# Earlier loads for the second MLP products, and recurrences placed inside w_o's first pass

## The chip, the cores and the metric

The kernel runs on one core of a Trainium2 chip. The core has a matrix engine (TensorE, PE in the profile; its weight loads are PEld), a vector engine (VectorE, DVE), a scalar engine (ScalarE, ACT), GpSimd (POOL) and SyncE (SP), which issues the DMAs here. The metric is the device time of one execution in microseconds. The kernel before takes 2242.0 us, the median of 3 runs (2241.39 to 2243.5).

## The reference

A trunk of two layers over a sequence of 1024 positions and a model width of 1024, all in float32:

```python
for layer in range(DEPTH):                      # DEPTH = 2
    h = rmsnorm(x, mix_norm_g[layer])
    if layer % 2 == 0:
        x = x + diff_attention(h, ...)          # layer 0
    else:
        x = x + recurrent_block(h, ...)         # layer 1
    x = x + sqrelu_mlp(rmsnorm(x, mlp_norm_g[layer]), mlp_w1[layer], mlp_w2[layer])
return rmsnorm(x, final_norm_g)

def sqrelu_mlp(h, w1, w2):                      # w1: 1024 x 4096, w2: 4096 x 1024
    return jnp.square(jax.nn.relu(h @ w1)) @ w2

def recurrent_block(h, ...):
    gate_branch = gelu(h @ w_y)
    xb = causal_depthwise_conv(h @ w_x, conv_w, conv_b)
    ...
    r, i = sigmoid(...), sigmoid(...)           # gates, block-diagonal products of xb
    log_a = -8.0 * r * softplus(-lam_param)
    a, mult = exp(log_a), sqrt(-expm1(2.0 * log_a))
    u = mult * (i * xb)
    _, hs = lax.associative_scan(_lru_combine, (a, u), axis=1)   # h_t = a_t h_(t-1) + u_t
    return (hs * gate_branch) @ w_o
```

## The kernel before

Every product of float32 matrices is made from rounded parts: each operand is split into a high part (ACT copies it to the rounded type, L342) and a low part (DVE subtracts, L345), and three matmuls (high x high, high x low, low x high) are added up in a result bank. A matmul here has 128 rows and columns of weights and 512 columns of data. Names ending in h and l are the parts: w2h and w2l, ysh and ysl.

The program's stages in the profiled execution are attention (until about 625 us), MLP of layer 0 (first product to 935, second product to about 1240), the recurrent block (to 1585), and the MLP of layer 1 (first product to 1902, second product and final norm to the end).

**The MLP's first product** (`mlp`) goes over 16 pairs of row blocks, `i` from 0 to 15. For each it forms seven products of half-size blocks, as in Strassen's scheme, 12 matmuls each, and DVE adds them up in the tiles ct and cl. The rest of a pair (`hidden_steps`) is done beside the next pair's products: ACT takes relu (rt, rl) and square (st, sl), DVE forms sums (h12, h34), and SP stores the seven half blocks as `hid[i]` to device memory: ct, two parts of cl, then h12 and two parts of h34. After the last pair these steps stand alone. In this stage the order on each engine is that of the code (`manual_schedule`).

**The second product** (`Second`) is cut into slots of 24 matmuls. Slots 0 to 7, of kind P, read half a block row of w2 (one DMA, L71) and two stored half blocks of hid (two DMAs, L91), and `prepare` splits both. `run` loads four slots ahead (AHEAD = 4) and prepares two ahead. Slots 0 and 1 are loaded at the start of pair 15 and prepared in it. In layer 1 the residual is kept transposed: `fetch_x` loads its eight blocks into xm, `turn_x` turns them with transposes on TensorE (L250) during slots 4 to 7, and ACT copies them out (L251). Layer 0 loads rows of x instead (L239).

**The recurrent block** works on pairs of 128 channels, n = 0 to 3. `lru` is the recurrence of one channel block: on ACT T = tanh, exp, sqrt and a copy with three functions that need table loads; on DVE two products, one more, and a scan along the sequence. The result times the gate branch is split into ys. At n = 3 the first pass of w_o is done with ys0 to ys3 (`out_group`: eight result blocks of 24 matmuls, two for each of four groups of w_o's columns), then both recurrences of the last pair, and then the second pass with ys4 to ys7 (L588 to L591), whose results are added to x (L1031) and passed block by block to the norm and splits of layer 1's first product (z, t12, t34, ssacc). Outside `manual_schedule` a scheduler of the framework orders the instructions of each engine.

SP issues the DMAs in its order, and each issue waits for the DMA eight issues before it.

Of the kernel before, what the change touches and what calls it, by code (L numbers as in the profile page):

```python
# [17 lines left out]
S = 1024  # L18
NK = D // P
# [275 lines left out]
class Trunk:  # L295
# [740 lines left out]
        if done is not None:  # L1036
            done(m)

    def out_group(self, blocks, w, r0, done=None, order=tuple(range(NK)), first=None, beside=()):

        nb = len(blocks)
        per = NK // nb
        wt = {} if first is None else {order[0] // per: first}
        beside = iter(beside)
        for m in order:
            g = m // per
            if g not in wt:
                wt[g] = self.w_out(w, r0, nb, g * per * P)
            for _ in self.out_block(blocks, wt[g], m, m % per, done=done):
                pass  # L1050
            next(beside, lambda: None)()

# [111 lines left out]
    def mlp(self, layer, last):  # L1164

        nc = self.nc
        mm = nc.tensor.matmul
        w1, w2 = self.ins["mlp_w1"][layer], self.ins["mlp_w2"][layer]
        self.hid = [self.dram.tile([P, 7, CH], F32, name=f"hid{layer}_{b}") for b in range(16)]
        l, r = slice(0, CH), slice(CH, S)
        box = {}

        def means():
            ps = self.acc1()  # L1180
            for j in range(NT):
                nc.tensor.matmul(ps[:, j : j + 1], self.ssacc[:, j * P : (j + 1) * P], self.ones, start=True, stop=True)
            inv = self.const.tile([P, NT], F32, name=f"inv{layer}")
            nc.vector.tensor_scalar(out=inv, in0=ps[:, :NT], scalar1=1.0 / D, scalar2=EPS, op0=ALU.mult, op1=ALU.add)
            nc.vector.reciprocal(out=inv, in_=inv)
            box["inv"] = inv
            self.ssacc = None

        def add(out, x, y, op=ALU.add):
            nc.vector.tensor_tensor(out=out, in0=x, in1=y, op=op)  # L1190

        with self.tc.manual_schedule(engines={EPE, EACT, EDVE, ESP}):
            second = self.second(w2, box, last)
            raws = self.pair_raws(w1, 1)
            before = {}
            for i in range(16):
                w = self.w
                new = {}
                if i + 1 < 16:
                    new, self.w = self.pair_weights(raws, i + 1)  # L1200
                if i + 2 < 16:
                    raws = self.pair_raws(w1, i + 2)
                if i == 15:
                    second.load(0)
                    second.load(1)
                    second.fetch_x(4)
                top, low = self.t4("ct"), self.t4("cl")
                p1, p67, p53 = self.acc1(), self.acc2(), self.acc2()
                p2, p4 = self.accg(), self.accg()

                def do(*names):
                    for name in names:
                        for steps in (new, before):
                            if name in steps:
                                steps[name]()

                def rows(a, b, bank, k):
                    (ah, al), (bh, bl) = w[a], self.sx[k][b]
                    mm(bank, ah[:, k], bh, start=k == 0, stop=False)  # L1219
                    mm(bank, ah[:, k], bl, start=False, stop=False)  # L1220
                    mm(bank, al[:, k], bh, start=False, stop=k == 3)  # L1221

                def product(a, b, bank):
                    for k in range(4 if i else 0):
                        rows(a, b, bank, k)

                if i == 0:

                    for k in range(4):
                        for at in (("A11", "B11", p1), ("S2", "T2", p67[:, l]), ("S1", "T1", p53[:, l]), ("S4", "B22", p53[:, r]),  # L1230
                                   ("S3", "T3", p67[:, r]), ("A12", "B21", p2), ("A22", "T4", p4)):
                            rows(*at, k)
                product("A11", "B11", p1)
                if "e6" in before:
                    before["e6"]()
                do("th", "s12", "rt", "st")
                product("S2", "T2", p67[:, l])
                nc.scalar.activation(out=top[:, l], in_=p1, func=AF.Copy)
                do("tl", "s34", "rl", "sl")
                product("S1", "T1", p53[:, l])  # L1240
                add(low[:, l], top[:, l], p67[:, l])
                do("h12", "lh", "t12", "l12")
                product("S4", "B22", p53[:, r])
                add(low[:, r], low[:, l], p53[:, l])
                do("h34", "t34", "l34")
                product("S3", "T3", p67[:, r])
                add(top[:, r], low[:, r], p53[:, r])
                do("ll")
                product("A12", "B21", p2)
                both = low.rearrange("p (h c) -> p h c", c=CH)  # L1250
                add(both, both, p67[:, None, r].to_broadcast([P, 2, CH]))
                if i == 2:
                    means()
                if i == 3:
                    box["q"] = box["inv"] if last else self.spread(box["inv"])
                if i == 15:
                    second.prepare(0)
                    second.prepare(1)
                product("A22", "T4", p4)
                add(top[:, l], top[:, l], p2)  # L1260
                before = self.hidden_steps(i, top, low, last)
                before["e6"] = lambda low=low, p4=p4: add(low[:, l], low[:, l], p4, ALU.subtract)
            for name in ("rt", "st", "e6", "rl", "sl", "t12", "t34"):
                before[name]()
            self.sx = None
            second.run()
# [134 lines left out]
    def recurrent(self, done):  # L1401
        nc, ins = self.nc, self.ins
        wx, wy, wo = ins["rec_w_x"][0], ins["rec_w_y"][0], ins["rec_w_o"][0]
        self.xg = self.new_xg
        rb = self.norm_later()
        self.x = [None] * NK
        ys, kept = {}, {}

        def back(c):
            parts = []  # L1410
            for p in range(2):
                t = self.t4("ys", F32R)
                nc.sync.dma_start(out=t.bitcast(F32), in_=kept[c][p])
                parts.append(t)
            return parts

        for n in range(4):
            rg = self.t4("raw", F32, (P, 2, 2, 256), "R")
            for gi, g in enumerate(("rec_w_a", "rec_w_i")):
                nc.sync.dma_start(out=rg[:, gi], in_=ins[g][0, n].rearrange("(k p) m -> p k m", p=P))  # L1420
            wg = self.split(rg, (P, 2, 2, 256), "wg")
            pair = (2 * n, 2 * n + 1)
            xbs, xss = zip(*[self.conv(wx, c, rb) for c in pair])
            gates = [self.gelu2(wy, c, rb) for c in pair]
            if n == 3:
                for c in range(4):
                    ys[c] = back(c)
            parts = []
            for j, c in enumerate(pair):
                sel = slice(j * P, (j + 1) * P)  # L1430
                r = self.gate(wg, 0, xss, sel, "r", self.vec("rec_b_a", c))
                ig = self.gate(wg, 1, xss, sel, "ig", self.vec("rec_b_i", c))
                parts.append((r, ig, c, xbs[j]))
            if n == 3:
                self.out_group([ys[c] for c in range(4)], wo, 0)
            hs = [self.lru(*p) for p in parts]
            for j, c in enumerate(pair):
                nc.vector.scalar_tensor_tensor(out=hs[j], in0=gates[j], scalar=0.5, in1=hs[j], op0=ALU.mult, op1=ALU.mult)
                ys[c] = self.split(hs[j], (P, S), "ys")
                if n < 2:  # L1440
                    kept[c] = [self.dram.tile([P, S], F32, name=f"y{c}{p}") for p in "hl"]
                    for t, d in zip(ys.pop(c), kept[c]):
                        nc.sync.dma_start(out=d, in_=t.bitcast(F32))
        self.out_group([ys[c] for c in range(4, 8)], wo, 512, done, beside=[lambda: self.mlp_first(1)])
        self.w_lo = None


# [83 lines left out]
```

## Time and profile before

| | |
|---|---|
| median of 3 runs | 2242.0 us (2241.39 to 2243.5) |
| profiled execution | 2248.95 us, span 2247.2 us |
| mean granted clock of TensorE | 0.981 |
| busy share of the span | PE 95%, DVE 68%, ACT 48%, POOL 4% |

The span is the time from the first to the last recorded instruction of the profiled execution; its own time is 1.75 us longer. An engine's row in a timeline gives start, duration, line, operation, output and inputs, and in brackets how long the engine had stood idle before it and what ended that. The durations of matmuls overlap: the next one starts before the last has ended. In a table of windows PEclk is the share of full clock that was granted.

### The profile page before, as it was taken

To read this page: it belongs to the slowest core of one execution; us is meant where nothing else is said; L and a number is where in the kernel's file an instruction comes from. 1 tells how busy PE (TensorE), PEld (TensorE's weight loads), DVE (VectorE), ACT (ScalarE), POOL (GpSimd) and SP (SyncE) were. 2 spreads that over 40 slices of the span, in tenths; PEclk is the share of its full clock that TensorE was granted. 3 is DMA by queue.
4 is the path that set the end of the run, shared out by engine and by line. 5 is a ranking of instruction groups with operands and counts; after the bars stand their busy time and mean duration, and the time that the engine had idled before them with its cause. 6 is when DMAs were issued, how large, how long until landed. Compare 5 with 4: busy or idle time off the path is not lost.

```text
span 2247.2 us, 26498 instructions
## 1 busy us (share of the span) xinstructions
PE 2130.8 (95%) x9826; PEld 1758.0 (78%) x9826; DVE 1530.5 (68%) x2073; ACT 1067.6 (48%) x1627; POOL 100.1 (4%) x171
## 2 busy tenths in 40 slices
PE   8997999879999999899999999999899999899997
PEld 7786777768888888788887887777688888688885
DVE  5465676565896777577878477756967776486575
ACT  4344566456663444344435266635644443453343
POOL 3201111110000000000000000000000000000000
PEclk9998999999999999999999999999999999999998
DMA  6635353453634443597647322144244444874633
GB/s 188 175 88 130 97 143 101 123 152 109 211 116 142 155 155 134 190 353 280 218 158 240 90 78 84 36 159 132 94 151 155 150 150 169 322 263 166 217 128 135
DMA packets 239298, 355.82 MB, mean 158 GB/s; under 512 B 16225, under 2 KB 137154, under 8 KB 239170
## 3 DMA queue, kind: packets, MB, share of 16 engines
q1 hardware_dynamic: 230338, 326.87, 43.6%
q0 software_dynamic: 7680, 25.17, 4.8%
q10 hardware_dynamic: 1152, 2.10, 0.3%
q8 instruction: 77, 1.26, 0.2%
q14 instruction: 51, 0.42, 0.1%
HBM read 229.29 MB, written 91.23 MB: 143 GB/s over the span
## 4 chain that ended last, share of the span: by engine, by line
PE 60%; DVE 11%; ACT 7%; issue 3%; DMA 2%; POOL 0%; SPq 0%; ACTq 0%; POOLq 0%; DVEq 0%
PE acc L1219 5%; PE acc L1220 5%; PE acc L1221 5%; PE acc L144 4%; PE acc L145 4%; PE acc L143 4%; PE acg L1219 2%; PE acg L1221 2%; PE acg L1220 2%; PE acc L589 2%; PE acc L588 2%; PE acb L145 2%; PE acb L143 2%; PE acb L144 2%; PE acg L145 2%
## 5 line engine op out<-in xcount | busy, mean ns | idle before, releaser
L1121 ACT ACTIVATE ct<-ct 128x1024 f32<-128x1024 f32 x64 | 67.9, 1061 | 251.1 <-DVE ct L1190 250.1
L345 DVE TENSOR_TENSOR h2l<-h,h2h 128x1024 fp32r<-128x1024 f32 x112 | 136.6, 1220 | 65.6 <-ACT h2h L342 61.9
L766 ACT ACTIVATE p<-acc,nmax 128x768 f32<-128x768 f32 (+7 forms) x128 | 95.3, 744 | 143.1 <-DVE nmax L783 71.5
L588 PE MATMUL acg<-xgh,wh 128*128 128x512 f32 x384 | 161.6, 421 | 1.5 <-ACT vT L732 1.5
L589 PE MATMUL acg<-xgl,wh 128*128 128x512 f32 x384 | 152.7, 398 | 0.0
L591 PE MATMUL acg<-xgh,wl 128*128 128x512 f32 x384 | 152.7, 398 | 0.0
L342 ACT ACTIVATE h2h<-h 128x1024 fp32r<-128x1024 f32 x112 | 117.6, 1050 | 59.6 <-DMA h<-hid 51.3
L342 ACT ACTIVATE w2h<-w 128x1024 fp32r<-128x1024 f32 x80 | 84.3, 1054 | 88.0 <-DVE w L56 72.1
L143 PE MATMUL acc<-w2h,h2h 128*128 128x512 f32 x256 | 103.0, 402 | 13.9 <-ACT w2h L342 12.2
L143 PE MATMUL acc<-h2h,w2h 128*128 128x512 f32 x256 | 101.1, 395 | 7.5 <-ACT w2h L342 7.4
L418 POOL TENSOR_TENSOR rstd<-ms,mhalf 128x4 f32<-128x4 f32 (+2 forms) x25 | 22.4, 897 | 1900.0 <-DVE ms L416 1898.6
L144 PE MATMUL acc<-w2l,h2h 128*128 128x512 f32 x256 | 102.3, 400 | 2.8 <-DVE w2l L345 2.8
L1220 PE MATMUL acc<-t12l,w12h 128*128 128x512 f32 x256 | 100.7, 393 | 4.4 <-DVE t12l L345 4.4
L1190 DVE TENSOR_TENSOR cl<-cl,acc 128x512 f32<-128x512 f32 x64 | 60.8, 950 | 64.3 <-PE acc L1221 64.3
L345 DVE TENSOR_TENSOR w2l<-w,w2h 128x1024 fp32r<-128x1024 f32 x80 | 97.7, 1222 | 9.0 <-PE acc L144 4.9
L145 PE MATMUL acc<-h2h,w2l 128*128 128x512 f32 x256 | 100.9, 394 | 2.7 <-DVE w2l L345 2.7
L1219 PE MATMUL acc<-t12h,w12h 128*128 128x512 f32 x256 | 100.6, 393 | 3.1 <-DVE ct L1190 3.1
L145 PE MATMUL acc<-w2h,h2l 128*128 128x512 f32 x256 | 101.5, 396 | 0.0
L144 PE MATMUL acc<-h2l,w2h 128*128 128x512 f32 x256 | 100.8, 394 | 0.0
L1221 PE MATMUL acc<-t12h,w12l 128*128 128x512 f32 x256 | 100.2, 391 | 0.0
L762 PE MATMUL acc<-ks,qs 128*128 128x512 f32 (+2 forms) x192 | 67.8, 360 | 23.0 <-DMA ks<-qkh 23.0
L591 PEld LDWEIGHTS acg<-xgh,wl 128*128 128x128 f32 x384 | 73.8, 192 | 17.0 <-DVE wl L345 0.5
(383 smaller groups left out, 6004.4 us busy)
## 6 DMA issues: line engine op xcount, KB each, us to landing
w<-in_mlp_w_dram SPq DMA_DIRECT2D x96, 512.0 KB, 4.4
raw<-in_mlp_w_dram SPq DMA_DIRECT2D x64, 512.0 KB, 4.4
h<-hid SPq DMA_DIRECT2D x64, 512.0 KB, 5.2
h<-hid SPq DMA_DIRECT2D x96, 256.0 KB, 5.1
w<-in_mlp_w_dram SPq DMA_DIRECT2D x80, 256.0 KB, 3.9
hid<-cl SPq DMA_DIRECT2D x64, 256.0 KB, 2.3
hid<-h SPq DMA_DIRECT2D x32, 512.0 KB, 2.6
hid<-h SPq DMA_DIRECT2D x64, 256.0 KB, 2.4
```

Source lines behind the costliest of these rows:

```text
L143: mm(bank[m], ah, bh, start=first, stop=False)
L144: mm(bank[m], ah, bl, start=False, stop=False)
L145: mm(bank[m], al, bh, start=False, stop=end)
L342: nc.scalar.activation(out=hi, in_=src, func=AF.Copy)
L345: (lo_eng or nc.vector).tensor_tensor(out=lo, in0=src, in1=hi.bitcast(F32), op=ALU.subtract)
L588: mm(ps[:, pc], a, xh[:, cs], start=(k == 0), stop=False)
L589: mm(ps[:, pc], a, xl[:, cs], start=False, stop=False)
L591: mm(ps[:, pc], b, xh[:, cs], start=False, stop=(k == n - 1))
L766: nc.scalar.activation(out=p[c][:, :n], in_=src, func=AF.Exp, bias=nmax[:, c : c + 1], accum_out=sums[:, c : c + 1])
L1219: mm(bank, ah[:, k], bh, start=k == 0, stop=False)
L1220: mm(bank, ah[:, k], bl, start=False, stop=False)
L1221: mm(bank, al[:, k], bh, start=False, stop=k == 3)
```

## The change

There are three edits. In `mlp` the loads of slots 2 and 3 are issued with pair 15's last steps, before its stores; `fetch_x(4)`, which loads xm0 to xm3 in layer 1, moves behind them; and slot 2 is prepared between pair 15's steps e6 and rl. In `recurrent`, at n = 3, the two recurrences are emitted after the first and the third result block of w_o's first pass. In `out_group`, the second pass is called with `late=2`: the first two result blocks, with another tag for their banks, do their products with ys4 and ys5 first, and those with ys6 and ys7 follow.

```diff
-    def out_group(self, blocks, w, r0, done=None, order=tuple(range(NK)), first=None, beside=()):
+    def out_group(self, blocks, w, r0, done=None, order=tuple(range(NK)), first=None, beside=(), late=0):
...
-            for _ in self.out_block(blocks, wt[g], m, m % per, done=done):
+            if late and m == order[0]:
+                two = [self.out_block(blocks, wt[g], n, n % per, done=done, tag="S") for n in order[:2]]
+                for steps in two:
+                    for _ in range(nb - late):
+                        next(steps)
+            steps = two.pop(0) if late and m in order[:2] else self.out_block(blocks, wt[g], m, m % per, done=done)
+            for _ in steps:
                 pass
...
                 if i == 15:
                     second.load(0)
                     second.load(1)
-                    second.fetch_x(4)
...
                 if i == 15:
                     second.prepare(0)
                     second.prepare(1)
+                    second.load(2)
+                    second.load(3)
+                    second.fetch_x(4)
...
-            for name in ("rt", "st", "e6", "rl", "sl", "t12", "t34"):
+            before["rt"]()
+            before["st"]()
+            before["e6"]()
+            second.prepare(2)
+            for name in ("rl", "sl", "t12", "t34"):
                 before[name]()
...
+            hs = []
+            recurrence = lambda: hs.append(self.lru(*parts[len(hs)]))
             if n == 3:
-                self.out_group([ys[c] for c in range(4)], wo, 0)
-            hs = [self.lru(*p) for p in parts]
+                self.out_group([ys[c] for c in range(4)], wo, 0, beside=[recurrence, lambda: None, recurrence])
+            else:
+                recurrence()
+                recurrence()
...
-        self.out_group([ys[c] for c in range(4, 8)], wo, 512, done, beside=[lambda: self.mlp_first(1)])
+        self.out_group([ys[c] for c in range(4, 8)], wo, 512, done, beside=[lambda: self.mlp_first(1)], late=2)
```

On ACT, around the end of layer 0's first product, the steps of pair 15 (ct, cl) and the splits of slot 2 (the first h2h and w2h after them) and slot 3 stood and stand as follows, the kernel before first:

```order
L1121 ACTIVATE ct_7941<-ct_7941 128x1024 x2
L1121 ACTIVATE cl_7942<-cl_7942 128x1024 x2
L342 ACTIVATE h2h_8105<-h_1308_8091 128x1024
L342 ACTIVATE w2h_8109<-w_1307_8090 128x1024
L342 ACTIVATE h2h_8144<-h_1310_8096 128x1024
```

Here slot 2's two splits stand behind both passes of cl, and slot 3's behind them. In the changed kernel the same place reads:

```order
L1130 ACTIVATE ct_7941<-ct_7941 128x1024 x2
L342 ACTIVATE h2h_8084<-h_1304_8059 128x1024
L342 ACTIVATE w2h_8088<-w_1303_8058 128x1024
L1130 ACTIVATE cl_7942<-cl_7942 128x1024 x2
L342 ACTIVATE h2h_8144<-h_1306_8064 128x1024
```

The two splits of slot 2 moved from behind cl to ahead of it; the count of instructions is the same.

On SP, at the end of layer 1's first product, the stores of pairs 14 and 15 (hid_14, hid_15) and the loads of slots 2, 3 and 4 (w, then two h) stood in this order before, where xm is the residual and gb the gain of the final norm:

```order
L232 DMA xm_14792<-x_0_12316 128x1024
...
L1127 DMA hid_14_12698<-ct_14647 128x512
...
L1127 DMA hid_15_12699<-h_2410_14942 128x512 x2
L1280 DMA gb_14949<-in_final_norm_g_dram 128x1024
L71 DMA w_2414_14951<-in_mlp_w_dram 128x2x512
...
L71 DMA w_2416_14956<-in_mlp_w_dram 128x2x512
...
L71 DMA w_2418_14961<-in_mlp_w_dram 128x2x512
...
L232 DMA xm_14974<-x_4_12320 128x1024
```

All three slots stand behind the stores of pair 15, and xm4 to xm7 behind the three slots. In the changed kernel the order is:

```order
L1136 DMA hid_14_12698<-h_2396_14862 128x512 x2
L71 DMA w_2405_14909<-in_mlp_w_dram 128x2x512
...
L71 DMA w_2407_14914<-in_mlp_w_dram 128x2x512
...
L232 DMA xm_14919<-x_0_12329 128x1024
...
L1136 DMA hid_15_12699<-ct_14792 128x512
...
L1295 DMA gb_14967<-in_final_norm_g_dram 128x1024
L71 DMA w_2422_14969<-in_mlp_w_dram 128x2x512
...
L232 DMA xm_14974<-x_4_12333 128x1024
```

Slots 2 and 3 and xm0 to xm3 now stand between the two groups of stores; slot 4 and xm4 to xm7 stay behind pair 15's.

On ACT, in w_o's first pass, T, r and w are tiles of the two recurrences (r_1944 the first, r_1948 the second), woh the split weights and ysh the split results. The kernel before, from the first split of the second pass's weights on:

```order
L342 ACTIVATE woh_2001_12286<-raw_2000_12284 128x1024
L1390 ACTIVATE T_1992_12252<-r_1944_11928,sp4_895 128x1024
L1391 ACT_TABLE_LOAD
...
L1390 ACTIVATE T_1994_12263<-r_1948_11958,sp4_895 128x1024
L342 ACTIVATE woh_2025_12398<-raw_2024_12396 128x1024
...
L1394 ACTIVATE T_1994_12263<-T_1994_12263 128x1024
L342 ACTIVATE ysh_1996_12275<-r_1944_11928 128x1024
L342 ACTIVATE ysh_1998_12280<-r_1948_11958 128x1024
```

The first recurrence begins only behind woh_2001, a weight of the second pass. In the changed kernel, where woh_1977 and woh_1987 are the third and fourth weight group of the first pass, the rows are:

```order
L1407 ACTIVATE w_1960_12026<-T_1959_12025 128x1024
L342 ACTIVATE woh_1977_12144<-raw_1976_12142 128x1024
L1409 ACTIVATE T_1959_12025<-T_1959_12025 128x1024
L1405 ACT_TABLE_LOAD
L1405 ACTIVATE T_1971_12102<-r_1948_11958,sp4_895 128x1024
...
L1409 ACTIVATE T_1971_12102<-T_1971_12102 128x1024
L342 ACTIVATE woh_1987_12210<-raw_1986_12208 128x1024
L342 ACTIVATE woh_2001_12286<-raw_2000_12284 128x1024
L342 ACTIVATE ysh_1996_12275<-r_1944_11928 128x1024
L342 ACTIVATE ysh_1998_12280<-r_1948_11958 128x1024
```

Both chains moved from behind the weights' splits into the first pass, the first ahead of its third weight group and the second ahead of its fourth.

## Rows read from the trace of the kernel before

**Rows 1.** The page's first part: busy time of each engine, share of the span and count of instructions.

```profile
PE 2130.8 (95%) x9826; PEld 1758.0 (78%) x9826; DVE 1530.5 (68%) x2073; ACT 1067.6 (48%) x1627; POOL 100.1 (4%) x171
```

**Rows 2.** TensorE's list of waits over the whole span: bank and line that waited, what ended it, then us in total, times, longest.

```profile
PE acc L143 <- ACT w2h L342: 19.6, 7, 9.0
...
PE acc L588 <- ACT ysh L342: 5.0, 1, 5.0
PE acc L1220 <- DVE t12l L345: 4.4, 3, 1.7
...
PE acc L1219 <- DVE ct L1190: 3.1, 2, 2.8
```

**Rows 3.** TensorE's timeline in layer 0's second product: its first matmul, the last one of slot 1, the first ones of slot 2 and of slot 8.

```profile
935.40 0.39 PE L143 MATMUL acc<-h2h,w2h 128*128 128x512 f32 x1
...
946.05 0.39 PE L145 MATMUL acc<-h2h,w2l 128*128 128x512 f32 x1
952.94 0.79 PE L143 MATMUL acc<-h2h,w2h 128*128 128x512 f32 x1 [6.50 <-ACT w2h L342]
...
988.56 0.39 PE L143 MATMUL acb<-h2h,w2h 128*128 128x512 f32 x1
```

**Rows 4.** ACT's timeline beside it: pair 15's cl, and the splits of slots 2, 4 and 5.

```profile
938.61 2.14 ACT L1121 ACTIVATE cl<-cl 128x1024 f32<-128x1024 f32 x2
950.89 1.06 ACT L342 ACTIVATE h2h<-h 128x1024 fp32r<-128x1024 f32 x1 [10.14 <-DMA h<-hid]
...
956.33 1.06 ACT L342 ACTIVATE h2h<-h 128x1024 fp32r<-128x1024 f32 x1 [0.70 <-DMA h<-hid]
...
960.33 1.06 ACT L342 ACTIVATE h2h<-h 128x1024 fp32r<-128x1024 f32 x1 [2.00 <-DMA h<-hid]
```

**Rows 5.** SP's timeline beside it: the last stores of pair 14, and the first load of slot 2.

```profile
924.52 5.16 SPq L1127 DMA_DIRECT2D hid<-h  x3
...
944.13 0.63 SPq L71 DMA_DIRECT2D w<-in_mlp_w_dram  x1
```

**Rows 6.** Windows of 2 us: busy time and instructions of each engine, then TensorE's granted clock, the DMA share and GB/s.

```profile
952.00:954.00 2.00, 1.06 (x2) 0.57 (x2) 2.00 (x2) 1.26 (x2) 0.00 (x0) 0.50 1.06 393
1618.00:1620.00 2.00, 2.00 (x6) 1.55 (x5) 1.97 (x4) 1.45 (x2) 0.00 (x0) 0.50 0.85 239
1918.00:1920.00 2.00, 0.00 (x0) 0.00 (x0) 0.00 (x0) 0.00 (x0) 0.00 (x0) 0.50 1.05 407
```

**Rows 7.** TensorE's timeline in w_o's passes: the second pass's first matmul, the last before its wait and the first after it, then the first matmul of layer 1's MLP and the one after that stage's last wait.

```profile
1534.56 0.39 PE L588 MATMUL acc<-ysh,woh 128*128 128x512 f32 x1
...
1542.49 0.39 PE L591 MATMUL acg<-ysh,wol 128*128 128x512 f32 x1
1547.85 1.22 PE L588 MATMUL acc<-ysh,woh 128*128 128x512 f32 x2 [4.97 <-ACT ysh L342]
...
1585.66 0.39 PE L1219 MATMUL acb<-b,wth 128*128 128x512 f32 x1
...
1616.30 0.47 PE L1219 MATMUL acc<-t12h,w12h 128*128 128x512 f32 x1 [2.76 <-DVE ct L1190]
```

**Rows 8.** ACT's timeline from the last gate of the recurrences on: two splits of w_o's weights, and the start of the first recurrence with its first table load and the pass behind it.

```profile
1491.23 1.12 ACT L1377 ACTIVATE ig<-acc,cols 128x1024 f32<-128x1024 f32 x1 [1.60 <-PE acc L591]
...
1513.71 1.06 ACT L342 ACTIVATE woh<-raw 128x1024 fp32r<-128x1024 f32 x1 [7.51 <-DMA raw<-in_rec_w_o_dram]
1523.42 1.06 ACT L342 ACTIVATE woh<-raw 128x1024 fp32r<-128x1024 f32 x1 [8.65 <-PE acc L589]
1524.39 1.14 ACT L1390 ACTIVATE T<-r,sp 128x1024 f32<-128x1024 f32 x1
1525.55 1.28 ACT L1391 ACT_TABLE_LOAD   x1
1526.84 1.15 ACT L1391 ACTIVATE r<-r,nsp 128x1024 f32<-128x1024 f32 x1
```

**Rows 9.** DVE's timeline behind it: the first results of the second pass, the last block's result, and the sum ct of layer 1's MLP.

```profile
1556.62 2.35 DVE L1031 TENSOR_TENSOR x<-x,acc 128x1024 f32<-128x1024 f32 x2 [3.11 <-PE acc L591]
...
1585.86 1.22 DVE L1031 TENSOR_TENSOR x<-x,acc 128x1024 f32<-128x1024 f32 x1
...
1615.48 0.68 DVE L1190 TENSOR_TENSOR ct<-cl,acc 128x512 f32<-128x512 f32 x1
```

**Rows 10.** TensorE's timeline in layer 1's second product: the first matmul, the first of slot 2, the first transposes of slot 4.

```profile
1902.78 0.39 PE L143 MATMUL acc<-w2h,h2h 128*128 128x512 f32 x1
...
1922.85 0.79 PE L143 MATMUL acc<-w2h,h2h 128*128 128x512 f32 x1 [9.03 <-ACT w2h L342]
...
1936.67 0.60 PE L250 MATMUL acb<-ident,xm 128*128 128x128 f32 x4
```

**Rows 11.** ACT's timeline beside it: the split of slot 2, and the first copy of a transposed block.

```profile
1920.80 1.06 ACT L342 ACTIVATE h2h<-h 128x1024 fp32r<-128x1024 f32 x1 [12.67 <-DMA h<-hid]
...
1938.68 0.58 ACT L251 ACTIVATE x<-acb 128x512 f32<-128x512 f32 x1
```

**Rows 12.** SP's timeline beside it: the last stores of pair 14, and the first load of slot 2.

```profile
1891.47 5.58 SPq L1127 DMA_DIRECT2D hid<-h  x3
...
1912.31 0.64 SPq L71 DMA_DIRECT2D w<-in_mlp_w_dram  x1
```

## Prediction

> **What bounds the kernel now.** I read the page's busy line first, then TensorE's list of waits, then the timeline around each long wait, and last the engine or queue that ended it. TensorE is busy 95% of the span [rows 1], so a change can win only where TensorE stands still or runs at half clock. Of the waits, three places are touched by the edits [rows 2]: L143 waiting for w2h (19.6 us in 7 waits, the start of the second MLP products), L588 waiting for ysh (5.0 us, w_o's second pass), and behind it L1220 waiting for t12l (4.4 us) and L1219 for ct.
>
> In both second products TensorE does the first two slots of 24 matmuls back to back and then stops until slot 2's weights are split: in layer 0 from 946.05 to 952.94, in layer 1 until 1922.85 after 9 us [rows 3, 10]. What ends it is ACT's h2h, which itself waited for a DMA [rows 4, 11]. That DMA was issued after pair 15's hid stores, at 944.13 and 1912.31 [rows 5, 12], though SP had finished pair 14's stores at 924.52 + 5.16 = 929.68. In w_o's second pass ACT starts the recurrences at 1524.39, after an early split of the next weights, and the first ysh releases TensorE at 1547.85, 5 us after it ran out of other matmuls at 1542.7 [rows 7, 8].
>
> Each such gap is paid twice. In the windows behind the two MLP gaps, and behind the 2.76 us wait at 1616.30, the granted clock stands at 0.50 of 2.4 GHz, that is 1.2 GHz, after TensorE had stood idle [rows 6]. So I count arrival times of a later matmul against the full pace, which contains both.
>
> **The change part by part.** The pace: 48 matmuls from 935.40 to 946.05, 47 steps, are 0.2266 us each, a slot of 24 is 5.44 us [rows 3].
>
> *A, layer 0's second product.* Slots 2 and 3 are now issued behind pair 14's stores, from 929.7, and their six DMAs have some nine us before pair 15's stores, the first of which waits for ACT's ct, done where cl starts at 938.61 [rows 4]. Slot 2's ACT work (h2h, w2h, 0.96 us apart) goes between ct and cl, so starts at about 938.6 [rows 4]; with the DVE halves it is ready near 942, slot 3 near 947. TensorE needs them at 946.3 and 951.7. Both wait no longer. Price of the move: cl and all of pair 15's stores go 2 x 0.96 = 1.9 us later, and slot 4 stands where slot 2 stood. Its h2h would then run at 950.89 + 1.9 = 952.8 and its w2l end near 956.3, against a need at 935.40 + 4 x 5.44 = 957.2. That is hidden by 0.9 us; uncovered it would cost the shortfall and perhaps a new half clock, 3 to 4 us. The slots after it come each 4.0 us (956.33 to 960.33, [rows 4]), faster than 5.44. So eight slots end at 935.40 + 43.5 = 978.9 in place of 988.56 [rows 3]: 9.7 us. Bounds 6 to 9.7.
>
> *B, the recurrences.* Same instructions, moved. ACT is free from 1491.23 + 1.12 = 1492.35, so the four ACT passes of each recurrence run beside the first pass of w_o. The second ysh needs no more than the split of woh before it (1523.42 in the rows of before), so both are ready near 1527 and their ysl near 1535. late=2 puts 24 matmuls on ys4 and ys5 first, which cover 1534.56 to 1540.0. Nothing is left to wait for, and 192 matmuls end at 1534.56 + 192 x 0.2266 = 1578.1 in place of 1585.66 [rows 7]: 7.6 us.
>
> What is late next is DVE. It is without a gap from 1556.62 to the ct that frees TensorE at 1616.30, 59.5 us of work [rows 9], and TensorE in that stretch loses 4.4 + 2.76 us [rows 2, 7]. With the first block finished after 36 matmuls, at 1542.7, DVE may start near 1543 and have that work done at 1602.6. The order also places about 6.4 us of it ahead of the last block's result, where 30.3 us (1585.86 to 1616.16) stood behind it, so from that side ct ends at 1578.3 + 24.6 = 1602.9. TensorE itself would arrive at 1616.30 - 2.76 - 4.4 - 7.6 = 1601.5. DVE's two limits coincide, so it has no slack while results come in one by one, and I take 3 us of remaining waits: 1604.6, a gain of 11.7, rounded to 11.5. Bounds: 7.5 (all those waits stay) to 15 (none stays).
>
> What the move costs in the first pass: the split of the fourth weight group, at 1513.71 [rows 8], now stands behind both chains on ACT. Adding the rows' durations, 4 table loads of 1.28 and eight passes of about 1.1, two of which (T of L1394) wait for DVE, it lands near 1515 and its wol near 1518.7. TensorE needs it two blocks before the end, at 1534.56 - 10.9 = 1523.7. It is covered by 5 us. The recurrences' passes on DVE (about 1.2 us each like the row at 1585.86, [rows 9]) delay results by up to 2 us; I count nothing, and what it costs if that is wrong is the slower rival.
>
> The trace has a table load from 1525.55 to 1526.83 and the next pass at 1526.84 [rows 8], so nothing follows the load. The Trainium skill (ScalarE: Activation LUTs, What ACT_TABLE_LOAD costs) adds a drain of about 1.38 us to each load. By that rule four loads would take some 5.5 us more and use up the 5 us of cover, and the sum would lose about 0.5 us; the row disagrees and I go by the row.
>
> *C, layer 1's second product.* The same move, with SP free from 1891.47 + 5.58 = 1897.05 [rows 12]. Unhindered, slot 4's transposes start at 1902.78 + 4 x 5.44 = 1924.5 in place of 1936.67 [rows 10]: 12.1 us. But these transposes read xm4 to xm7, which are queued behind pair 15's stores (now 1.9 us later), the final gain and slot 4. Slot 4 takes slot 2's place: 1920.80 + 1.9 = 1922.7 [rows 11]. Four xm are 2.1 MB; at the 407 GB/s of a full window [rows 6] 5.2 us, so they land at 1927.9. TensorE does the xm0 to xm3 quarter (0.44 us) and waits about 3.0. Slot 5's transposes need the banks that ACT's copies (1938.68 in before, behind the next slot's splits, [rows 11]) empty: another 1.5. I take 12.1 - 3.0 - 1.5 = 7.6. Bounds: 12.1 if the data is early, and 3 if TensorE waits twice for 3 us and falls to half clock once more for about 3.
>
> At 407 GB/s the row says that loads can run near that rate. The Trainium skill (DMA: Bandwidth & Descriptors, Where 436 GB/s comes from) has loads from HBM bound at about 358 GB/s. By that rule the xm would land 0.7 us later and C would be 6.9; the row disagrees.
>
> Sum: 9.7 + 11.5 + 7.6 = 28.8 us. Against the profiled execution (2248.95 us, span 2247.2) that is 2220. The median of the runs is 2242.0, 7 us under it; the same amount taken from it gives 2213.
>
> **The rivals.**
> *The wait moves to the DMAs.* For: from 942 and from 1910 on the queues are full (share 1.05 in the window, [rows 6]), and nothing is removed from them. Against: slots are used at 1.05 MB per 5.44 us, half of what the row moves. If slot 4 and the xm are late, A falls to 6, C to 3, and the sum to 20.5: 2221.5.
> *DVE sets the end of B.* For: its 59.5 us without a gap. Against: the order moves work ahead of the last block. If all 30.3 us stay behind it, B is 7.6 and the sum 24.9: 2217.
> *Slower: the recurrences hold up the first pass.* One mechanism: on ACT's queue the split of the fourth weight group waits for the two chains, on DVE the results wait behind the scans. Price: the chains took 29.1 us in before, from T at 1524.39 to 1553.5, where DVE's 3.11 us of idle time before 1556.62 begin [rows 8, 9]. TensorE begins to pay beyond 5 us of delay. If it stood for all of it and 3 us of half clock, B would be 11.5 - 32 = -20.5, and with A and C as forecast the time 2242.0 - 17.3 + 20.5 = 2245; with A and C at 9 together, 2253. For it: the one-engine queues. Against: ACT was idle 7.5 and 8.7 us before the two splits there [rows 8].
> *The loads come no earlier,* since their buffers or slot 2's h wait for something of pair 15: then A and C vanish and a B at its lower end of 7.5 with its stores 2 us late gives 2236; if B fails too, no change.
>
> **How the numbers follow.** Forecast 0.60 (2213, own range 2208 to 2218), DMA 0.20, DVE 0.12, loads no earlier 0.05, slower 0.03. With A 6, B 7.5, C 3 the sum is 16.5 and the time 2225.5; with 9.7, 15 and 12.1 it is 36.8 and 2205. The range is 2205 to 2227. A difference below 0.2%, 4.5 us, is what a measurement of this kernel can't tell from none. Faster 0.94, within 0.03, slower 0.03.
>
> **What would show it.** In the profile after: L143's wait for w2h gone from the 5 to 10 us class in both layers; slot 8 of layer 0 starting 43.5 us after the first matmul; L588's wait for ysh gone and T of L1405 near 1492 relative to the same first pass; a DVE wait at t12l or ct still there, under 4 us; a wait of about 3 us at the transposes of L250. Wrong would be: a new wait at L589 or L591 for wol in the first pass, a wait for w2h at slot 4, or a granted clock of 0.50 at new places.

## The result and the profile after

The changed kernel takes 2217.94 us, the median of 4 runs (2216.23 to 2222.5), against 2242.75 us of the kernel before (4 runs, 2241.39 to 2243.67). The ratio is 0.9893, 95% interval 0.9876 to 0.991. The forecast was 2213, in a range of 2205 to 2227: right in direction and within the range, 5 us optimistic by this median. The same kernel was timed twice more, each time beside the kernel before: 2214.19 us beside 2246.09 (0.9859, interval 0.9836 to 0.9882) and 2217.05 beside 2245.92 (0.9871, 0.9857 to 0.9886). The three gains are 24.8, 31.9 and 28.9 us; forecast were 28.8.

TensorE's list of waits in the changed kernel (bank and line that waited, what ended it, us in total, times, longest), to be laid beside [rows 2]; L1227 and L1228 are L1219 and L1220 of before:

```profile
PE acc L143 <- ACT w2h L342: 4.1, 4, 1.5
PE acc L1227 <- DVE ct L1199: 3.1, 2, 2.8
...
PE acg L250 <- DMA xm<-x: 1.7, 2, 1.0
...
PE acc L1228 <- DVE t12l L345: 0.3, 1, 0.3
```

The wait for ysh is gone, and with it those for t12l but for 0.3 us. L143's wait fell from 19.6 to 4.1 us, its longest from 9.0 to 1.5; what is left of it stands at the end of both second products, where before had it too. New is L250's wait for xm. The wait for ct is what it was.

TensorE's timeline of the changed kernel, answering to [rows 3], [rows 7] and [rows 10]:

```profile
938.68 0.39 PE L143 MATMUL acc<-h2h,w2h 128*128 128x512 f32 x1
...
949.56 0.39 PE L143 MATMUL acc<-h2h,w2h 128*128 128x512 f32 x1
...
982.20 0.39 PE L143 MATMUL acb<-h2h,w2h 128*128 128x512 f32 x1
...
1531.13 0.39 PE L588 MATMUL acc<-ysh,woh 128*128 128x512 f32 x1
...
1574.65 0.39 PE L1227 MATMUL acb<-b,wth 128*128 128x512 f32 x1
...
1600.26 0.77 PE L1227 MATMUL acc<-t12h,w12h 128*128 128x512 f32 x1 [2.80 <-DVE ct L1199]
...
1887.94 0.39 PE L143 MATMUL acc<-w2h,h2h 128*128 128x512 f32 x1
...
1909.71 0.60 PE L250 MATMUL acb<-ident,xm 128*128 128x128 f32 x4
1910.14 0.38 PE L250 MATMUL acg<-ident,xm 128*128 128x128 f32 x2
1911.25 0.33 PE L250 MATMUL acg<-ident,xm 128*128 128x128 f32 x1 [0.72 <-DMA xm<-x]
1912.53 0.33 PE L250 MATMUL acg<-ident,xm 128*128 128x128 f32 x1 [0.95 <-DMA xm<-x]
...
1913.49 0.74 PE L143 MATMUL acc<-w2h,h2h 128*128 128x512 f32 x1
...
1920.64 0.60 PE L250 MATMUL acb<-ident,xm 128*128 128x128 f32 x4
```

Slot 2 of layer 0 follows slot 1 at 949.56 without a gap, and slot 8 comes 982.20 - 938.68 = 43.52 us after the first matmul. The second pass of w_o runs through in 1574.65 - 1531.13 = 43.52 us. In layer 1 TensorE reaches slot 4 after 1909.71 - 1887.94 = 21.77 us, where before needed 33.89 [rows 10]; then it waits for xm.

Laid end to end, the starts of such first matmuls cut the span into stages. Here they are for the profile before and for all three profiles of the changed kernel (us; "on" is from slot 8 to slot 51, "rest" what follows it, in layer 0 up to the last matmul of the stage, at 1266 in the profile before and not near 1240 as the outline of the kernel has it):

| stage | before | after | second | third |
|---|---|---|---|---|
| attention | 626.5 | 629.8 | 627.0 | 627.2 |
| layer 0, first product | 308.9 | 308.9 | 308.9 | 308.9 |
| second product to slot 8 | 53.2 | 43.5 | 43.5 | 43.5 |
| on | 233.9 | 233.9 | 233.9 | 233.9 |
| rest of it | 43.8 | 46.7 | 43.9 | 44.1 |
| recurrent block | 319.4 | 311.9 | 311.9 | 313.4 |
| layer 1, first product | 317.1 | 313.3 | 310.5 | 312.1 |
| second product to slot 8 | 62.8 | 54.5 | 54.7 | 54.1 |
| on | 235.6 | 235.6 | 235.6 | 235.6 |
| rest | 46.0 | 42.7 | 42.8 | 42.7 |

Four stages carry the gain: 9.6, 7.6, 3.8 and 8.3 us in the first profile, 29.3 in all. The first profile's span fell by 26.5 alone, since attention took 3.3 us longer, the rest of layer 0 2.9 longer, and the end 3.3 less, all three in instructions that the change does not move. The end has 42.7 or 42.8 us in all three profiles of the changed kernel, but that is not the change's either: the kernels below with the moved recurrences alone and with `late=2` alone, which keep the old `mlp`, have 42.8 too, and the one with all xm early has 46.0. In the profile before, the granted clock stood at 0.50 there from 2216 to 2224 us.

### The profile page after: what moved, and what is told of

Same layout as the page of the kernel before. It is cut to its first block, busy times and chain, and to the rows that moved or that the text cites. A ratio compares the mean times of both kernels' runs of the same rounds, so it can differ in the third digit from the quotient of the medians.

```text
span 2220.7 us, 26499 instructions
## 1 busy us (share of the span) xinstructions
PE 2128.3 (96%) x9826; PEld 1759.9 (79%) x9826; DVE 1529.8 (69%) x2073; ACT 1066.6 (48%) x1627; POOL 100.1 (5%) x171
## 4 chain that ended last, share of the span: by engine, by line
PE 69%; DVE 13%; ACT 9%; DMA 4%; issue 4%; POOL 1%; SPq 0%; ACTq 0%; POOLq 0%; DVEq 0%
PE acc L1227 5%; PE acc L1228 5%; PE acc L1229 5%; PE acc L145 4%; PE acc L143 4%; PE acc L144 4%; PE acg L588 3%; PE acg L589 3%; PE acg L591 3%; PE acg L1227 2%; PE acg L1229 2%; PE acg L1228 2%; PE acb L819 2%; PE acb L145 2%; PE acb L143 2%
## 5 line engine op out<-in xcount | busy, mean ns | idle before, releaser
L345 DVE TENSOR_TENSOR h2l<-h,h2h 128x1024 fp32r<-128x1024 f32 x112 | 136.6, 1219 | 56.8 <-ACT h2h L342 50.9
L143 PE MATMUL acc<-w2h,h2h 128*128 128x512 f32 x256 | 101.9, 398 | 4.0 <-ACT w2h L342 2.3
L345 DVE TENSOR_TENSOR w2l<-w,w2h 128x1024 fp32r<-128x1024 f32 x80 | 97.7, 1221 | 10.8 <-PE acc L144 4.9
L1227 PE MATMUL acc<-t12h,w12h 128*128 128x512 f32 x256 | 101.0, 395 | 3.1 <-DVE ct L1199 3.1
L143 PE MATMUL acc<-h2h,w2h 128*128 128x512 f32 x256 | 100.5, 393 | 1.9 <-ACT w2h L342 1.8
L1228 PE MATMUL acc<-t12l,w12h 128*128 128x512 f32 x256 | 100.9, 394 | 0.3 <-DVE t12l L345 0.3
```

What stands on the lines that cost most here:

```text
L143: mm(bank[m], ah, bh, start=first, stop=False)
L345: (lo_eng or nc.vector).tensor_tensor(out=lo, in0=src, in1=hi.bitcast(F32), op=ALU.subtract)
```

## The experiments

**Each half alone.** The first kernel has the edits of `mlp` and the old recurrent block, the second the reverse.

> Only the edits in mlp; the recurrent block as in the kernel before. My theory (the steps add up, each place by itself): slot 8 of layer 0's second product comes 9.6 us and that of layer 1's 8.3 us sooner after its first matmul, as in the changed kernel, the wait for ysh of 5.0 and the three for t12l stay; 17.9 us less, 2224. Rival (the timed gain of the whole, 24.8 us, is 4.5 smaller than the 29.3 of the trace's steps because the loads are late only beside the profiler's own traffic): 13 us less, 2229.

> Only the edits in the recurrent block (recurrences moved, late=2); mlp as before. My theory: the second pass of w_o ends 7.6 us sooner and layer 1's first product loses 3.8 us less, 11.4 us in all, 2231, and about 3 us of wait at ct stay since DVE is without a gap there. Rival (the loads' share is small and the recurrences carry the gain): 15 us or more, 2227.

Measured, beside 2245.55 us of the kernel before (17 runs, 2241.8 to 2250.7): 2232.93 us with `mlp` alone, ratio 0.9943 (0.9929 to 0.9957), and 2235.0 with the recurrent block alone, 0.9953 (0.9939 to 0.9967). By stages the first has 43.5 and 54.3 us to slot 8 and the old 319.1 and 317.1 between; the second has 52.6 and 62.1 to slot 8 and 311.9 and 312.0 between. So each edit works in its own place and the steps add up in the trace, as the first theory had it. The timed gains do not add up as well: 12.6 and 10.5 us, where the stages say 18.2 and 12.7. By its time `mlp` alone lies at the rival's 13 us and not at the theory's 17.9; the rival's cause, loads that are late only beside the profiler's traffic, was not tested by itself. Of the 5.6 us that `mlp` alone lacks, 3.4 are the height at which the profiled execution of before lay over the median of those 17 runs (2248.95 against 2245.55), and 1.7 are attention, 628.2 us in this kernel's profile against 626.5. Whether the timed executions without a stage table differ in the same places stays open.

TensorE's timeline of the kernel with `mlp` alone shows both stalls of the old recurrent block, and a wait at slot 5's transposes that the changed kernel's first profile does not have:

```profile
1540.04 1.09 PE L588 MATMUL acc<-ysh,woh 128*128 128x512 f32 x2 [4.97 <-ACT ysh L342]
...
1608.11 0.47 PE L1227 MATMUL acc<-t12h,w12h 128*128 128x512 f32 x1 [2.80 <-DVE ct L1199]
...
1918.87 0.33 PE L250 MATMUL acg<-ident,xm 128*128 128x128 f32 x1 [0.95 <-DMA xm<-x]
...
1926.91 0.66 PE L250 MATMUL acb<-ident,xm 128*128 128x128 f32 x4 [1.35 <-ACT x L251]
```

The last row is the wait for ACT's copies that the prediction put at 1.5 us. The changed kernel's second and third profiles have it too, with 1.34 and 1.36. In its first profile the clock had fallen to 0.50 behind the xm wait, slot 4 took 7.15 us (1913.49 to 1920.64), and the copies were in time.

**The parts of the recurrent edit.** One kernel keeps the moved recurrences and drops `late=2`, the other keeps `late=2` and puts the recurrences back; `mlp` is as before in both.

```diff
-        self.out_group(..., done, beside=[lambda: self.mlp_first(1)], late=2)
+        self.out_group(..., done, beside=[lambda: self.mlp_first(1)])
```

> As the kernel with only the recurrent edits, but without late=2: the blocks of the second pass are done one after another as the scheduler likes. Theory that moving the recurrences does it: no wait for ysh over 1 us, first result at most as late, so 2231 or up to 2.7 us less, since the first block then needs 24 matmuls and not 36 before its result. Rival (the split results come only near 1535 and late=2 is what covers them): a wait of 1 to 4 us at L588 or L589, 2233 to 2236.

> late=2 alone, the recurrences where they were. Theory: the second pass has 24 matmuls ahead of the first that needs ysh, where the scheduler had found 36; the wait grows from 5.0 to about 7.7 us and the time to about 2245. Rival (late=2 is worth something by itself, since the scheduler adds to it): the wait is 5.0 or less, 2242 or below.

Measured: 2233.8 us without `late=2`, 0.9948 (0.9933 to 0.9963), and 2244.78 with `late=2` alone, 0.9998 (0.9986 to 1.0009). Without `late=2` no wait for ysh or ysl is left; the stages are 311.8 and 310.0, where both edits together gave 311.9 and 312.0. The one new wait is 0.86 us for a result bank. So moving the recurrences does it, and `late=2` is not needed once they are moved. With `late=2` alone the wait is longer, as the 24 matmuls against 36 said, in the list of waits of that kernel:

```profile
PE acc L588 <- ACT ysh L342: 7.7, 1, 7.7
```

Its recurrent block takes 324.8 us, 5.4 more than before, and the first product of layer 1 311.9, 5.2 less: the time lost in waiting for ysh is time in which DVE catches up, and the t12l waits vanish. That is why the whole stays where it was, not the 3 us slower that I expected.

**What holds ct.** The sums of squares go to GpSimd in one kernel, whose diff this is, and are left out in another.

```diff
-            nc.vector.tensor_tensor(out=self.ssacc, in0=self.ssacc, in1=sq, op=ALU.add)
+            nc.gpsimd.tensor_tensor(out=self.ssacc, in0=self.ssacc, in1=sq, op=ALU.add)
```

> The changed kernel with the sums of squares (L530, 7 passes of 1.14 us in each layer's norm) on GpSimd in place of VectorE. Theory (after the second pass DVE's 59.5 us without a gap set the end): ct comes up to 8 us earlier from DVE's side, so the wait of 2.8 us at ct goes and with it the half clock behind it, about 4 us less than the changed kernel. Rival (the ct wait hangs on ACT or on TensorE's own order): it stays at 2.8, no gain. A loss is possible if GpSimd's passes, 2.4 to 3.1 us each by like rows, slow DVE's.

> The changed kernel without the seven sums of squares of each layer's norm (L530 left out, so the norm uses the first block's squares alone). Theory (DVE's work without a gap holds ct): 7 x 1.14 = 8 us of it are gone, ct's wait of 2.8 us goes to under 0.5 and layer 1's first product takes about 307.5 us in place of 310.5 to 313.3; 3 to 6 us less than the changed kernel. Rival (the wait hangs on something else, and the 3 to 6 us that GpSimd's version lost were not DVE's being held up): it stays near 2.8.

On GpSimd: 2223.34 us, ratio to before 0.9901 (0.9883 to 0.9919), 9 us slower than the changed kernel timed beside it (2214.19). VectorE's and GpSimd's timelines of that kernel show why:

```profile
1568.54 2.57 POOL L530 TENSOR_TENSOR ssacc<-ssacc,sq 128x1024 f32<-128x1024 f32 x1 [7.97 <-ACT sq L529]
1576.18 3.45 POOL L530 TENSOR_TENSOR ssacc<-ssacc,sq 128x1024 f32<-128x1024 f32 x1 [5.07 <-ACT sq L529]
```

```profile
1567.62 1.22 DVE L345 TENSOR_TENSOR t12l<-t,t12h 128x1024 fp32r<-128x1024 f32 x1
1568.76 3.43 DVE L345 TENSOR_TENSOR t34l<-t,t34h 128x1024 fp32r<-128x1024 f32 x1
...
1576.18 1.22 DVE L345 TENSOR_TENSOR t12l<-t,t12h 128x1024 fp32r<-128x1024 f32 x1
1577.32 0.68 DVE L1031 TENSOR_TENSOR x<-x,acg 128x512 f32<-128x512 f32 x1
1577.92 2.79 DVE L345 TENSOR_TENSOR t34l<-t,t34h 128x1024 fp32r<-128x1024 f32 x1
```

The two VectorE passes t34l that meet GpSimd's take 3.43 and 2.79 us in place of 1.22, so the 1.14 us that moved came back with more, and TensorE waited 3.55 us at a new place for a result bank. Layer 0's first product, where the sums moved too, took 313.4 us in place of 308.9, with a wait of 2.52 us of the same kind, and layer 1's 316.4. That test did not decide the question. Leaving the sums out did: 2210.08 us, 0.9841 (0.9825 to 0.9857), 7 us under the changed kernel timed beside it (2217.05), and the wait at ct is this, in TensorE's timeline:

```profile
1589.16 0.47 PE L1226 MATMUL acc<-t12h,w12h 128*128 128x512 f32 x1 [0.33 <-DVE ct L1198]
```

0.33 in place of 2.8 us, with layer 1's first product in 307.1 us (expected 307.5). Taking 8 us from VectorE takes the wait away, so VectorE's queue holds ct.

**What holds slot 4 in layer 1.** Three kernels: the early preparation of slot 2 left out; all xm ahead of pair 15's stores; and slot 4 ahead of them as well. The diff is that of the last.

```diff
                     second.load(3)
-                    second.fetch_x(4)
+                    second.load(4)
+                    second.fetch_x(8)
```

> The changed kernel without the early prepare of slot 2: loads as there, the splits of slot 2 behind cl and pair 15's sums, as run() places them. Theory (loads give the gain, the early split only the last part): slot 2's weights are split near 946.5 in layer 0, so a wait of 0.5 to 1.5 us at slot 2 in each layer; pair 15's stores and with them slot 4 and xm come 1.9 us earlier, so the xm wait of 1.7 goes; within 2 us of the changed kernel. Rival (the early split is needed): waits of 3 us or more and half clock behind them, 4 us or more slower than the changed kernel.

> The changed kernel with xm4 to xm7 loaded beside xm0 to xm3, ahead of pair 15's stores. Theory (the transposes of slot 4 wait for xm4 to xm7, which stand behind those stores, and the half clock follows from that wait): no wait at L250 for xm, no window at 0.50 behind it, slot 8 of layer 1 after about 51 us in place of 54.5, 2 to 4 us less than the changed kernel; a wait of about 1.4 us at slot 5 for ACT's copies may come in its place. Rival (the DMAs are the limit there): the same wait at L143 for slot 4's weights, no gain.

> The changed kernel with slot 4 and all eight xm loaded ahead of pair 15's stores. Theory (in the run with only xm early, slot 4's weights took the place of the xm as what comes last behind pair 15's stores): neither wait is left, slot 8 of layer 1 comes 43.5 + 4 x 1.67 = 50.2 us after the first matmul in place of 54.5, about 4 us less than the changed kernel; layer 0 unchanged at 43.5. Rival (the queues stay full, so pair 15's stores and slots 5 to 7 come late in turn): a wait at slot 5 or 6, 54 us or more.

Without the early split: 2217.45 us, 0.9876 (0.9857 to 0.9895). Slot 2 does not wait in either layer: layer 0's slot 8 comes after 43.5 us as before. Pair 15's stores are 1.9 us earlier, one of the two xm waits goes, and slot 8 of layer 1 comes after 53.9 us. By the stages the early split can be left out; I had expected a wait of 0.5 to 1.5. The time does not settle it: this kernel is 3.3 us slower than the changed kernel timed beside it (2214.19). In the profiles that lies in the recurrent block (313.8 us against 311.9) and layer 1's first product (312.1 against 310.5), neither of which this edit touches, and the changed kernel's third profile has 313.4 and 312.1 there.

With all xm early: 2219.91 us, 0.9886 (0.9867 to 0.9905), 5.7 us slower than the changed kernel timed beside it. In the profiles 0.6 us of that stand at slot 8 (55.3 us against 54.7) and 3.2 at the end (46.0 against 42.8), which this edit does not touch. The xm wait is gone, and TensorE's timeline has this where the products of slot 4 begin:

```profile
1903.17 0.60 PE L250 MATMUL acg<-ident,xm 128*128 128x128 f32 x4
1905.34 0.50 PE L143 MATMUL acc<-w2h,h2h 128*128 128x512 f32 x1 [1.57 <-ACT w2h L342]
1906.79 0.50 PE L144 MATMUL acc<-w2l,h2h 128*128 128x512 f32 x1 [0.95 <-DVE w2l L345]
```

The transposes run through, and slot 4's weights come 2.5 us late in their place. With slot 4 early too: 2216.75 us, 0.9865 (0.9842 to 0.9887), against 2217.05 of the changed kernel timed beside it, the same. Now TensorE goes through slot 4 and stops at the next, and ACT's timeline beside it shows for what:

```profile
1912.66 0.66 PE L250 MATMUL acb<-ident,xm 128*128 128x128 f32 x4 [2.40 <-ACT x L251]
```

```profile
1907.42 1.06 ACT L342 ACTIVATE h2h<-h 128x1024 fp32r<-128x1024 f32 x1 [15.26 <-DMA h<-hid]
...
1910.12 1.06 ACT L342 ACTIVATE h2h<-h 128x1024 fp32r<-128x1024 f32 x1 [0.69 <-DMA h<-hid]
1911.09 1.04 ACT L342 ACTIVATE w2h<-w 128x1024 fp32r<-128x1024 f32 x1
1912.03 0.58 ACT L251 ACTIVATE x<-acb 128x512 f32<-128x512 f32 x1
```

The copies that free the banks stand on ACT behind the splits of slots 5 and 6, and those wait for their data. Slot 5's split starts 26.3 us after the stage's first matmul, in the changed kernel 27.4: slot 4 and all xm go ahead of slot 5 in both, so it comes only 1 us earlier, while TensorE comes to slot 5 3.7 us earlier. Slot 8 comes after 55.3 us with xm early, 54.9 with slot 4 early too, and 54.1 to 54.7 in the changed kernel. Counted in waits alone, 2.5 and 2.4 us are about 1 us less than the changed kernel's 2.1 + 1.34; the clock, which fell to half behind both (0.50 in the windows of 1908 to 1910 and of 1914 to 1916 us), took that back. The rival came nearer: the DMA share is 1.03 to 1.07 in these windows, so the queue is full, and each order chooses who waits.

**Together, and the changed kernel again.** One kernel has slot 4 and all xm early, no early split and no `late=2`; the other two are the changed kernel itself.

> As the one with slot 4 and all xm early, and in addition without late=2 and without the early prepare of slot 2. By the stages of the runs with each alone: layer 1's first product 310.0 (0.4 to 3 us less), second product to slot 8 50.2 (4.3 less), layer 0 43.5: 5 to 7 us less than the changed kernel, 2208 to 2212. Rival (the parts get in each other's way, slot 2's late split now missing its place): not below the changed kernel.

> The changed kernel once more, for a second trace of the same instructions. If the steps are properties of the kernel, slot 8 of layer 0 comes again 43.5 us after the first matmul, the wait at ct is again 2.8 and the xm wait about 1.7; if the 2.9 us lost in layer 0's tail and the 3.3 won in layer 1's are chance, they change or go (tail of layer 0 43.8 in place of 46.7 us). The time is 2216 to 2222, 24 to 29 us under the kernel before of the same chip.

> The changed kernel a third time, on the chip of the last three, to compare them with. The steps as before: 43.5 us to slot 8 in layer 0, a wait of 2.8 at ct, 54.5 to 54.7 us to slot 8 in layer 1; which of the half clocks behind the small waits fall is chance, so 2213 to 2221.

The combination takes 2218.36 us, 0.9873 (0.9853 to 0.9893), the same as the changed kernel timed beside it (2217.05), where 5 to 7 us less were expected. Slot 8 of layer 1 came after 53.5 us and not 50.2, with a wait of 2.42 us for ACT's copies, and the first product took 311.6 us and not 310.0: no better version came out. Of the repeats, the first is faster than expected, 2214.19 us where 2216 to 2222 were. The rest of layer 0 went back to 43.9 us, so the 2.9 us lost there were chance; the second repeat lies within its range. They gave the times at the top and two columns of the table.

## Why the prediction was right, point by point

*A.* Forecast 9.7, measured 9.64 in every profile of the changed kernel, beside the profile before; three other kernels with the old `mlp` take 52.4 to 53.0 us to slot 8, which would make it 8.9 to 9.4. Slot 4's split, which was to start 1.9 us after slot 2's of before, starts 1.5 us after it, in ACT's timeline of the changed kernel:

```profile
939.83 2.15 ACT L1130 ACTIVATE ct<-ct 128x1024 f32<-128x1024 f32 x2 [10.84 <-DVE ct L1199]
941.88 1.04 ACT L342 ACTIVATE h2h<-h 128x1024 fp32r<-128x1024 f32 x1
...
943.78 2.14 ACT L1130 ACTIVATE cl<-cl 128x1024 f32<-128x1024 f32 x2
...
955.69 1.06 ACT L342 ACTIVATE h2h<-h 128x1024 fp32r<-128x1024 f32 x1 [7.87 <-DMA h<-hid]
```

All is 938.68 - 935.40 = 3.28 us later here than in the profile before; 955.69 less that is 952.4, forecast 952.8. The cover of 0.9 us held.

*B, first half.* Forecast 7.6, measured 7.6 and 7.5 in the first two profiles and 6.0 in the third. ACT's timeline, 3.45 us earlier here than before (1487.78 against 1491.23 for the last gate):

```profile
1487.78 1.12 ACT L1392 ACTIVATE ig<-acc,cols 128x1024 f32<-128x1024 f32 x1 [1.59 <-PE acc L591]
1488.79 1.14 ACT L1405 ACTIVATE T<-r,sp 128x1024 f32<-128x1024 f32 x1
1489.95 1.28 ACT L1406 ACT_TABLE_LOAD   x1
1491.24 1.15 ACT L1406 ACTIVATE r<-r,nsp 128x1024 f32<-128x1024 f32 x1
...
1511.80 1.04 ACT L342 ACTIVATE woh<-raw 128x1024 fp32r<-128x1024 f32 x1
1523.36 1.06 ACT L342 ACTIVATE woh<-raw 128x1024 fp32r<-128x1024 f32 x1 [10.52 <-DMA raw<-in_rec_w_o_dram]
1524.33 1.99 ACT L342 ACTIVATE ysh<-r 128x1024 fp32r<-128x1024 f32 x2
```

The fourth weight group's split stands at 1511.80 + 3.45 = 1515.3, forecast near 1515, and no matmul of the first pass waits for it. The slower rival, which lived on that split, is out. Again a pass follows the table load at once, 0.01 us behind it in all 22 loads of this profile.

*B, second half.* Forecast 3.9 with 3 us of waits left; measured 3.8 in the first profile, with 2.80 + 0.30 left, and 6.6 and 5.0 in the others with the same waits; that the first came so near is luck. The named cause holds: VectorE's timeline has no gap from 1542.54, a little behind the first result, to ct.

```profile
1539.49 1.22 DVE L1031 TENSOR_TENSOR x<-x,acc 128x1024 f32<-128x1024 f32 x1 [5.16 <-PE acc L591]
...
1542.54 1.21 DVE L1031 TENSOR_TENSOR x<-x,acc 128x1024 f32<-128x1024 f32 x1
...
1575.59 0.68 DVE L1031 TENSOR_TENSOR x<-x,acg 128x512 f32<-128x512 f32 x1
...
1599.44 0.68 DVE L1199 TENSOR_TENSOR ct<-cl,acc 128x512 f32<-128x512 f32 x1
```

From the last block's result to ct's end are 1600.12 - 1575.59 = 24.5 us; 24.6 were counted from the order. The run without the sums of squares confirmed the cause. The whole of B, 11.4, moves between 11.0 and 14.1 in the three profiles, mostly with the half clock behind the waits.

*C.* Forecast 7.6, measured 8.3, 8.1 and 8.7. The unhindered 12.1 is there (33.89 less 21.77 us to slot 4). Slot 4's split was forecast at 1922.7 and xm at 1927.9; ACT's timeline has the split:

```profile
1907.47 1.06 ACT L342 ACTIVATE h2h<-h 128x1024 fp32r<-128x1024 f32 x1 [10.39 <-DMA h<-hid]
```

With the 14.84 us by which this stage stands earlier, 1907.47 and, for the last wait for xm, 1912.53 are 1922.3 and 1927.4. The xm wait was mis-sized: the transposes took 1913.49 - 1909.71 = 3.78 us in place of 1.67, 2.1 us lost and not 3.0, since six of the eight xm had landed when TensorE came to them, and it waited only for the last two. The second loss, 1.5 us for ACT's copies, is there with 1.34 to 1.36 us in three profiles; in the first one the clock took 1.7 us in its place (7.15 us for slot 4 against 5.44), so there this term came out by luck, by a cause that was not the one named. Waits and clock together cost C 12.1 - 8.3 = 3.8 us, forecast 4.5; the DMA rival had 9.1, and took 3.7 from A, which lost nothing.

*The sum.* 28.8 was forecast, the stages give 29.3, 31.9 and 29.4, the timed medians 24.8, 31.9 and 28.9. In the first profile, whose span fell by 26.5 us, the shortfall is not in any step. It lies in stages that the change does not touch; attention alone took 624.2 to 629.8 us in the profiles of this case. That the first timed median falls short for the same reason is not shown, since the timed executions have no stage table.

*What the prediction named as signs of being wrong.* Two did not come: no wait for wol in the first pass, none for w2h at slot 4. The third did in the first profile, a granted clock of 0.50 at new places, behind the xm wait and in the rest of layer 0; the second and third have it at neither. One reading was off: the window of 1918 to 1920 us in [rows 6] lies inside layer 1's gap, with TensorE at 0.00, and not behind it. That the gap is paid twice stands even so, since the first matmul behind it took 0.79 us in place of 0.39 [rows 10].

## What to carry to other kernels

A gap at the matrix engine is priced by the arrival of a later matmul at full pace, because the clock, where it falls in the gap, is paid too; and before a gain is booked, the next engine in line is counted from the same event (here 59.5 us of VectorE without a gap), since that sets what is left of it. Where the DMA queue is full, an earlier place for one load is a later place for another: look whose wait follows. And two single profiles of a kernel with small waits differ by several us in stages of equal instructions, so steps are compared stage by stage, not by spans.

## What the runs showed of the hardware

A pass on GpSimd and a VectorE pass that meet can hold each other up, and either may be the one that waits. In the kernel with the sums on GpSimd, VectorE's t34l rose from 1.22 to 3.43 and 2.79 us for 128x1024, while t12l at 1576.18 kept its 1.22 us. In layer 0 GpSimd's pass was held up in its turn: here it took 8.16 us, in place of the 2.4 of its shortest, over eight VectorE passes, of which only the last was lengthened (to 3.29 us):

```profile
634.38 8.16 POOL L530 TENSOR_TENSOR ssacc<-ssacc,sq 128x1024 f32<-128x1024 f32 x1 [5.74 <-ACT sq L529]
```

Passes that read a result bank keep their length: L1031 at 1577.32 takes its 0.68 us inside GpSimd's pass of 1576.18 to 1579.63, and six others of L1031 that overlap one of GpSimd's take the usual 0.68 or 1.22. The Trainium skill (GPSIMD Engine Reference, Specifications) says that GpSimd shares its interfaces to the on-chip memory with VectorE and meets it in instructions with two inputs from there. The rows agree: L345 has two such inputs, L1031 one.

The clock falls behind the same small wait in one execution and not in another. Windows of 2 us behind the ct wait, in the first profile of the changed kernel and then in its second (columns as in [rows 6]):

```profile
1600.00:1602.00 2.00, 1.74 (x4) 1.48 (x5) 2.00 (x4) 0.00 (x0) 0.00 (x0) 0.50 0.04 12
1602.00:1604.00 2.00, 2.00 (x6) 1.52 (x6) 1.97 (x4) 1.49 (x2) 0.00 (x0) 0.50 0.87 239
```

```profile
1594.00:1596.00 2.00, 1.17 (x5) 1.02 (x6) 2.00 (x4) 0.00 (x0) 0.00 (x0) 1.00 0.03 8
1596.00:1598.00 2.00, 2.00 (x10) 1.63 (x10) 2.00 (x4) 0.95 (x1) 0.00 (x0) 1.00 0.57 155
```

The waits were 2.80 and 2.77 us; the stage took 313.3 and 310.5. The 2.9 us that the first profile lost in the rest of layer 0 are the same thing behind waits of 0.2 to 1.1 us: the granted clock there was 0.50 (1.2 GHz) in this window, and 1.00 throughout in the profile before.

```profile
1232.00:1234.00 2.00, 1.78 (x4) 1.17 (x4) 1.29 (x2) 1.08 (x2) 0.00 (x0) 0.50 0.69 205
```
